# Column means of an 8192 x 8192 array: two-row loads up to group 59, another set of early blocks, and a last row group in four other pieces

## The chip, the cores and the metric

The kernel runs on one core of a Trainium2 chip. The time is the device time of one execution in microseconds (us); the runs shown are separate executions of the same program. The profile is one profiled execution of that program, with times counted from its first instruction.

The engines are named as the profile names them: PE is TensorE (PEld is its weight load), DVE is VectorE, ACT is ScalarE, POOL is GpSimd and SP is SyncE. A "q" behind the name, as in SPq, is the engine's instruction queue, where it waits or issues transfers.

## The reference

```python
def setup_inputs():
    return {"x": np.random.randn(8192, 8192).astype(np.float32)}

def reference(x):
    return np.mean(x, axis=0)
```

The input has 268 MB in fp32, the output 32 KB. Every element is read once and added.

## The kernel before

The 8192 rows are 64 *row groups* of 128 rows each, numbered 0 to 63 (the variable `g`); one row group fills the 128 partitions and has 8192 columns, cut into 16 *blocks* of `F = 512` columns. `W = 128` is a quarter of a block. A tile `bufs` holds six row groups: slots 0 to 3 take the loads in turn, slot 4 is called `both` and slot 5 `acc`.

**Loads.** SyncE issues all loads, in program order, from one queue; `load` (L75) sends one off as soon as the reader of its target slot has ended. First come two blocks of row group 60 into the tile `early`, then row groups 0 to 3 in one load, 4 and 5 in one load straight into `both` and `acc`, and five blocks of row group 63 into `early`. Row groups 6 to 55 are loaded in pairs, 56 to 59 one at a time, 60 with its first 14 blocks, 61 and 62 whole, and of row group 63 what is left in four pieces: blocks 4 to 7, 0 to 3, 14 and 15, and 8.

**Adds.** VectorE adds (`add`, L94; the instruction is L96). For a pair it writes the sum of both row groups to `both` and adds that to `acc`: two adds of 8192 columns. For a single row group it adds straight to `acc`. A no-op on ScalarE or GpSimd (L99) waits for the load and the add before it on VectorE's behalf, so that VectorE has one wait only. From row group 61, VectorE adds blocks 7 to 15 alone; row group 62 it does not add at all. GpSimd adds the early blocks to `acc` behind row groups 24 and 32 (L129) and three blocks of row group 62 at the end (L148).

**Products.** The sum over the 128 partitions is made by TensorE: a matmul with a 128 x 32 matrix of 1/8192 (`ones`) gives the column means of up to 512 columns. Block `i` goes to the 32-column strip `i % 4` of the array and to PSUM tile `banks[i // 4]`, so that four blocks can run on the four strips side by side. What was not added to `acc` is summed in PSUM: products of `acc`, row groups 61, 62 and 63 for the same columns go to the same place. The list `sums` gives their order, which is kept. Blocks 9 to 13, 14 and 15, and 8 are cut over all four strips (`spread`) into the PSUM tiles `wide`, `two` and `last`. There are 63 products.

**End.** ScalarE copies the PSUM tiles to `both` (L198), VectorE copies `last` to `tail` (L214). Five stores (L201) write the output, two of them issued by ScalarE and three by SyncE, the last one of `tail`. `landed` (L69) makes SyncE wait for loads and stores ahead of the end.

Of the kernel before, what the change touches and what calls it, by code (L numbers as in the profile page):

```python
# [9 lines left out]
def kernel(  # L10
# [2 lines left out]
    x: bass.AP,  # L13
    out: bass.AP,
):

    nc = tc.nc
    f32 = mybir.dt.float32
    M, N = x.shape  # L40
    P = nc.NUM_PARTITIONS
    F = 512
    W = F // 4
    G = M // P
    U = 6
    sync = mybir.DependencyInfo(mybir.DependencyClass.Sync, mybir.DependencyReason.DATA)

    sb = ctx.enter_context(tc.tile_pool(name="sb", bufs=1))
    psp = ctx.enter_context(tc.tile_pool(name="psum", bufs=1, space=bass.MemoryType.PSUM))
# [2 lines left out]
    both = bufs[:, U - 2, :]  # L52
    acc = bufs[:, U - 1, :]
    ones = sb.tile([P, 32], f32, name="ones")
    early = sb.tile([P, 7 * F], f32, name="early")
    tail = sb.tile([P, W], f32, name="tail")
    warm = sb.tile([P, 32], f32, name="warm")
    nc.gpsimd.memset(ones[:], 1.0 / M)  # L58
    ready = sb.tile([P, 1], f32, name="ready")
    tc.keep_in_program_order(  # L60
        nc.gpsimd.tensor_add(out=ready[:], in0=ones[:, 0:1], in1=ones[:, 1:2]))  # L61
    banks = [psp.tile([P, F], f32, name=f"bank{b}") for b in range(2)]
    wide = psp.tile([P, 2 * F], f32, name="wide")
    two = psp.tile([P, 2 * W], f32, name="two")
    last = psp.tile([P, W], f32, name="last")

    loads = []
# [1 line left out]
    def landed(*inss):  # L69

        nop = tc.keep_in_program_order(nc.sync.nop()).ins
        for o in inss:
            tc.add_manual_dep(nop, o.name, sync, reason="SyncE waits")

    def load(dst, src):  # L75
        ins = tc.keep_in_program_order(nc.sync.dma_start(out=dst, in_=src)).ins  # L76
        k = len(loads)
        over = loads[k - 8:k - 6] if k >= 8 and k % 2 == 0 else []
        tc.declare_no_dep(ins, group="loads", keep=over, reason="the reader of the buffer waited")
        for o in over:  # L80
            tc.add_manual_dep(ins, o.name, sync, reason="covers the next load too")
        tc.add_to_no_dep_group("loads", ins)
        loads.append(ins)
        return ins

    def rows(g, n=1):
        return x[g * P:(g + n) * P, :]

    def load_rows(g, u, n):
        return load(bufs[:, u:u + n, :], rows(g, n).rearrange("(p j) c -> p j c", j=n))  # L90
# [2 lines left out]

    def add(dst, a, b, dmas):  # L94

        ins = nc.vector.tensor_add(out=dst, in0=a, in1=b).ins  # L96
        if dmas and adds:
            waiter = nc.scalar if len(adds) % 8 > 1 else nc.gpsimd
            nop = joins[waiter] = tc.keep_in_program_order(waiter.nop()).ins  # L99
            for o in dmas + adds[-1:]:  # L100
                tc.add_manual_dep(nop, o.name, sync, reason="the no-op waits")
            for group in ("loads", "adds"):
                tc.declare_no_dep(ins, group=group, reason="the no-op waited")
            tc.add_manual_dep(ins, nop.name, sync, reason="waits for both at once")
        elif adds:
            tc.declare_no_dep(ins, group="loads", reason="the add ahead waited")
        tc.declare_no_dep(ins, group="early", reason="the no-op waited, or the add behind it")
        tc.add_to_no_dep_group("adds", ins)
        adds.append(ins)

    load(early[:, 5 * F:], rows(G - 4)[:, 14 * F:])
    first, second = load_rows(0, 0, 4), load_rows(4, 4, 2)
    load(early[:, :5 * F], rows(G - 1)[:, 9 * F:14 * F])
    add(bufs[:, 2:4, :], bufs[:, 2:4, :], bufs[:, 0:2, :], [first])
    add(bufs[:, 4:6, :], bufs[:, 4:6, :], bufs[:, 2:4, :], [second])
    add(acc, acc, both, [])
    tc.keep_in_program_order(nc.scalar.copy(out=warm[:], in_=ones[:]))  # L117
    ahead = []
    g = 6
    while g < G - 8:  # L120
        u = (g + 2) % 4
        dma = load_rows(g, u, 2)
        add(both, bufs[:, u, :], bufs[:, u + 1, :], [dma])
        add(acc, acc, both, ahead)
        ahead = []
        if g in (24, 32):
            lo, hi = (0, 4) if g == 24 else (4, 7)
            cols = slice((9 + lo) * F, (9 + hi) * F)
            ins = tc.keep_in_program_order(nc.gpsimd.tensor_add(  # L129
                out=acc[:, cols], in0=acc[:, cols], in1=early[:, lo * F:hi * F])).ins  # L130
            tc.add_to_no_dep_group("early", ins)
            ahead = [ins]
        g += 2

    while g < G - 4:
        row = bufs[:, (g + 2) % 4, :]
        add(acc, acc, row, [load(row, rows(g))])
        g += 1
    for lo, hi, loaded in [(0, 14, 14), (7, 16, 16)]:
        row = bufs[:, (g + 2) % 4, :]  # L140
        dma = load(row[:, :loaded * F], rows(g)[:, :loaded * F])
        cols = slice(lo * F, hi * F)
        add(acc[:, cols], acc[:, cols], row[:, cols], [dma])
        g += 1
    r61, r62, r63 = [bufs[:, (g + 1 + j) % 4, :] for j in range(3)]
    load(r62, rows(g))
    for cols in [slice(14 * F, 16 * F), slice(8 * F, 9 * F)]:
        joined = tc.keep_in_program_order(nc.gpsimd.tensor_add(  # L148
            out=acc[:, cols], in0=acc[:, cols], in1=r62[:, cols])).ins
    g += 1  # L150
    for lo, hi in [(4, 8), (0, 4), (14, 16), (8, 9)]:
        load(r63[:, lo * F:hi * F], rows(g)[:, lo * F:hi * F])

    sums = []

    def blocks(row, lo, hi):
        for i in range(lo, hi):
            sums.append((banks[i // 4], i % 4, 0, row[:, i * F:(i + 1) * F]))

    def spread(dst, row, lo, hi, part=slice(None)):  # L160
        n = (hi - lo) * W
        for c in range(0, n, F)[part]:
            for q in range(4):
                at = lo * F + q * n + c
                sums.append((dst, q, c, row[:, at:at + min(F, n - c)]))

    blocks(acc, 2, 5)
    blocks(acc, 0, 2)
    blocks(r61, 0, 7)
    blocks(acc, 5, 8)  # L170
    blocks(r62, 0, 8)
    spread(wide, acc, 9, 14, slice(1))
    blocks(r63, 4, 8)
    spread(wide, r62, 9, 14, slice(1))
    for row in (acc, r62):
        spread(wide, row, 9, 14, slice(1, 2))
    spread(two, acc, 14, 16)
    blocks(r63, 0, 4)
    spread(last, acc, 8, 9)
    spread(two, r63, 14, 16)  # L180
    spread(last, r63, 8, 9)
    for n, (dst, q, c, cols) in enumerate(sums):
        summed = tc.keep_in_program_order(nc.tensor.matmul(  # L183
            out=dst[32 * q:32 * q + 32, c:c + cols.shape[1]],
            lhsT=ones[:],
            rhs=cols,
            start=all((d is dst, k, at) != (True, q, c) for d, k, at, _ in sums[:n]),
            stop=all((d is dst, k, at) != (True, q, c) for d, k, at, _ in sums[n + 1:]),
            tile_position=(0, 32 * q),
            skip_group_check=True,  # L190
        )).ins

    res = both[:, :2 * F].rearrange("p (b c) -> p b c", b=2)
    res5 = both[:, 2 * F:2 * F + 5 * W]
    res2 = both[:, 4 * F:4 * F + 2 * W]

    def copy(dst, src):
        return tc.keep_in_program_order(nc.scalar.copy(out=dst, in_=src)).ins  # L198

    def store(engine, dst, src, *then):  # L200
        ins = tc.keep_in_program_order(engine.dma_start(out=dst, in_=src)).ins  # L201
        for o in then:
            tc.add_manual_dep(ins, o.name, sync, reason="follows that load")
        return ins

    def part(lo, hi):
        return out[lo * F:hi * F].rearrange("(q c) -> q c", q=4)

    copy(res[:, 1, :], banks[1][:])
    s1 = store(nc.scalar, part(4, 8), res[0:P:32, 1, :], loads[-4])  # L210
    copy(res5, wide[:, :5 * W])
    copy(res[:, 0, :], banks[0][:])
    copied = copy(res2, two[:])
    ended = nc.vector.tensor_copy(out=tail[:], in_=last[:]).ins  # L214
    landed(*joins.values())
    s5 = store(nc.sync, part(9, 14), res5[0:P:32, :], *loads[-7:-3])
    s0 = store(nc.sync, part(0, 4), res[0:P:32, 0, :])
    s2 = store(nc.scalar, part(14, 16), res2[0:P:32, :])
    store(nc.sync, part(8, 9), tail[0:P:32, :])
    landed(loads[-2], joined)  # L220
    landed(loads[-1], copied)
    landed(s0, s5)
    landed(s1, summed)
    landed(s2, ended)
    hold = tc.keep_in_program_order(nc.vector.nop()).ins
    tc.add_manual_dep(hold, s0.name, sync, reason="VectorE ends late")

# [29 lines left out]
```

## Time and profile before

| | us |
|---|---|
| median of 3 runs | 628.49 |
| lowest and highest | 628.24, 628.56 |
| span of the profiled execution, first to last instruction | 626.4 |
| median minus that span | 2.1 |
| VectorE busy | 529.3 (85%) |
| TensorE busy | 13.3 (2%) |
| HBM read | 268.44 MB, 429 GB/s over the span |

The profile does not list a device time of the profiled execution beside its span; the runs' median stands in for it. The table gives averages over the whole span. The busy share of an engine says how much work it has, not when the work can begin; the order of the last 80 us is read in the timeline, and the chain of waits says what ended last. DMA engines are busy in every slice of the page.

### The profile page before, as it was taken

The numbers are of one execution on the slowest core, as the hardware profiler recorded it, in microseconds if no ns is written. First come the engines' busy times: TensorE is split into PE (matmuls) and PEld (weight loads), VectorE is DVE, ScalarE is ACT, GpSimd is POOL, SyncE is SP. The second block draws the span as 40 slices with busy tenths as digits, with TensorE's granted clock in tenths as the row PEclk, the third lists the DMA queues.
The fourth block names the chain that finished last, engine by engine and source line by source line (L and its number), as shares of the span: only waits on it lengthen the run. The fifth ranks groups of instructions, "written<-read, shape, count | busy, mean of one in ns | idle before, by whom it ended". The sixth has DMA issues, their size and how long they took to land.

```text
span 626.4 us, 484 instructions
## 1 busy us (share of the span) xinstructions
PE 13.3 (2%) x126; PEld 4.0 (1%) x126; DVE 529.3 (85%) x60; ACT 3.7 (1%) x6; POOL 12.0 (2%) x10
## 2 busy tenths in 40 slices
PE   0000000000000000000000000000000000000008
PEld 0000000000000000000000000000000000000002
DVE  0028999998888998889998899888898888999992
ACT  0000000000000000000000000000000000000001
POOL 0000000000000000020000200000000000000002
PEclk9999999999999999999999999999999999999999
DMA  8999999999999999999999999999999999999997
GB/s 372 465 402 428 459 410 460 402 469 402 469 402 469 402 469 402 469 402 469 402 465 406 439 431 427 444 410 460 402 469 402 469 402 469 402 435 435 419 435 305
DMA packets 5930, 268.50 MB, mean 429 GB/s; under 512 B 660, under 2 KB 668, under 8 KB 1064
## 3 DMA queue, kind: packets, MB, share of 16 engines
q1 hardware_dynamic: 5912, 268.46, 99.3%
q8 instruction: 1, 0.02, 0.0%
q10 hardware_dynamic: 16, 0.01, 0.0%
q14 instruction: 1, 0.01, 0.0%
HBM read 268.44 MB, written 0.03 MB: 429 GB/s over the span
## 4 chain that ended last, share of the span: by engine, by line
DMA 59%; DVE 30%; another core or an unknown queue 10%; issue 0%; SPq 0%; ACTq 0%; PE 0%; POOL 0%; POOLq 0%
DMA bufs<-in_x_dram 59%; DVE bufs L96 30%; SPq L76 0%; ACTq L99 0%; PE last L183 0%; DVE tail L214 0%; POOL ready L61 0%; POOL ones L58 0%; POOLq L99 0%; POOLq L241 0%
## 5 line engine op out<-in xcount | busy, mean ns | idle before, releaser
L96 DVE TENSOR_TENSOR bufs<-bufs 128x8192 f32<-128x8192 f32 (+3 forms) x59 | 529.0, 8966 | 85.9 <-DMA bufs<-in_x_dram 43.0
L183 PE MATMUL bank<-bufs,ones 128*32 128x512 f32 x62 | 10.0, 716 | 610.3 <-DVE bufs L96 610.0
L129 POOL TENSOR_TENSOR bufs<-bufs,early 128x2048 f32<-128x2048 f32 (+1 forms) x2 | 7.9, 3954 | 348.5 <-DVE bufs L96 348.5
L148 POOL TENSOR_TENSOR bufs<-bufs 128x1024 f32<-128x1024 f32 (+1 forms) x2 | 3.6, 1824 | 258.9 <-DMA bufs<-in_x_dram 258.9
L214 DVE COPY tail<-last 128x128 f32<-128x128 f32 x1 | 0.3, 291 | 8.8 <-PE last L183 8.8
L183 PEld LDWEIGHTS bank<-bufs,ones 128*32 128x32 f32 x62 | 2.2, 121 | 616.4 <-issue 614.5
L198 ACT COPY bufs<-bank 128x512 f32<-128x512 f32 x2 | 1.2, 586 | 617.9 <-PE bank L183 617.9
L183 PE MATMUL wide<-bufs,ones 128*32 128x512 f32 (+1 forms) x32 | 2.5, 432 | 0.0
L117 ACT ACT_TABLE_LOAD x1 | 1.3, 1283 | 0.7 <-PEq L241 0.7
L183 PE MATMUL two<-bufs,ones 128*32 128x256 f32 x16 | 1.2, 380 | 0.0
L183 PEld LDWEIGHTS wide<-bufs,ones 128*32 128x32 f32 x32 | 1.0, 110 | 1.8 <-issue 1.8
L183 PE MATMUL last<-bufs,ones 128*32 128x128 f32 x16 | 0.8, 279 | 0.1
L198 ACT COPY bufs<-wide 128x640 f32<-128x640 f32 x1 | 0.7, 692 | 1.1 <-PE wide L183 1.1
L183 PEld LDWEIGHTS last<-bufs,ones 128*32 128x32 f32 x16 | 0.4, 109 | 1.2 <-issue 0.6
L183 PEld LDWEIGHTS two<-bufs,ones 128*32 128x32 f32 x16 | 0.4, 109 | 0.1
L198 ACT COPY bufs<-two 128x256 f32<-128x256 f32 x1 | 0.4, 372 | 0.1
L117 ACT COPY warm<-ones 128x32 f32<-128x32 f32 x1 | 0.2, 217 | 0.0
L61 POOL TENSOR_TENSOR ready<-ones 128x1 f32<-128x1 f32 x1 | 0.2, 193 | 0.1
L58 POOL MEMSET ones<- 128x32 f32 x1 | 0.1, 125 | 0.3 <-POOLq L241 0.3
L241 POOL MEMSET const-float32-0.0<- 128x1 f32 x1 | 0.1, 98 | 0.2 <-issue 0.2
L241 POOL MEMSET const-bfloat16-1.0<- 128x1 bf16 x1 | 0.1, 102 | 0.0
L241 POOL MEMSET const-uint8-127<- 128x1 uint8 x1 | 0.1, 102 | 0.0
(1 smaller groups left out, 0.1 us busy)
## 6 DMA issues: line engine op xcount, KB each, us to landing
bufs<-in_x_dram SPq DMA_DIRECT2D x6, 4096.0 KB, 20.4
bufs<-in_x_dram SPq DMA_DIRECT2D x1, 3584.0 KB
bufs<-in_x_dram SPq DMA_DIRECT2D x2, 1024.0 KB, 18.7
early<-in_x_dram SPq DMA_DIRECT2D x1, 1280.0 KB
early<-in_x_dram SPq DMA_DIRECT2D x1, 512.0 KB
bufs<-in_x_dram SPq DMA_DIRECT2D x1, 512.0 KB, 19.4
bufs<-in_x_dram SPq DMA_DIRECT2D x27, 29.9
bufs<-in_x_dram SPq DMA_DIRECT2D x1, 256.0 KB, 19.7
```

Of the source, the lines that this page charges most:

```text
L58: nc.gpsimd.memset(ones[:], 1.0 / M)
L61: nc.gpsimd.tensor_add(out=ready[:], in0=ones[:, 0:1], in1=ones[:, 1:2]))
L96: ins = nc.vector.tensor_add(out=dst, in0=a, in1=b).ins
L117: tc.keep_in_program_order(nc.scalar.copy(out=warm[:], in_=ones[:]))
L129: ins = tc.keep_in_program_order(nc.gpsimd.tensor_add(out=acc[:, cols], in0=acc[:, cols], in1=early[:, lo * F:hi * F])).ins
L148: joined = tc.keep_in_program_order(nc.gpsimd.tensor_add(out=acc[:, cols], in0=acc[:, cols], in1=r62[:, cols])).ins
L183: summed = tc.keep_in_program_order(nc.tensor.matmul(out=dst[32 * q:32 * q + 32, c:c + cols.shape[1]], lhsT=ones[:], rhs=cols, start=all(( ...
L198: return tc.keep_in_program_order(nc.scalar.copy(out=dst, in_=src)).ins
L214: ended = nc.vector.tensor_copy(out=tail[:], in_=last[:]).ins
L241: nc = _bacc.Bacc("TRN2", target_bir_lowering=False, num_devices=1)
```

## The change

Loads: the early blocks are the first six of row group 61 (two ahead of everything, four behind row group 5). Row groups 0 and 1 are loaded into `both` and `acc`, and all further ones up to 59 as pairs; row group 60 whole and alone; of row group 61 the ten blocks left; 62 whole; 63 whole, in pieces of 8, 4, 3 and 1 blocks.

Adds: row groups 2 and 3, then 4 and 5, are added as pairs of 16384 columns onto `both` and `acc`. Row groups 60 and (its ten blocks) 61 are added to `acc`; 62 and 63 are not added. GpSimd adds two early blocks behind row group 24, four behind 32, and none at the end.

Products: row group 62, then `acc`, then row group 63, with 16 blocks each; blocks 0 to 14 whole into four `banks`, block 15 as four quarters into `last`. These are 57 products.

End: four ScalarE copies, of the banks in order (the fourth with 96 partitions), one VectorE copy of `last`, and three stores, all by SyncE: 12 blocks, 3 blocks, 1 block. The waits of SyncE for loads stand partly ahead of the stores.

The diff, cut to its core:

```diff
-    early = sb.tile([P, 7 * F], f32, name="early")
+    E = 6
+    early = sb.tile([P, E * F], f32, name="early")
...
-    banks = [psp.tile([P, F], f32, name=f"bank{b}") for b in range(2)]
-    wide = psp.tile([P, 2 * F], f32, name="wide")
-    two = psp.tile([P, 2 * W], f32, name="two")
+    banks = [psp.tile([P, F], f32, name=f"bank{b}") for b in range(4)]
...
-    load(early[:, 5 * F:], rows(G - 4)[:, 14 * F:])
-    first, second = load_rows(0, 0, 4), load_rows(4, 4, 2)
-    load(early[:, :5 * F], rows(G - 1)[:, 9 * F:14 * F])
-    add(bufs[:, 2:4, :], bufs[:, 2:4, :], bufs[:, 0:2, :], [first])
-    add(bufs[:, 4:6, :], bufs[:, 4:6, :], bufs[:, 2:4, :], [second])
-    add(acc, acc, both, [])
+    def load_early(lo, hi):
+        load(early[:, lo * F:hi * F], rows(G - 3)[:, lo * F:hi * F])
+
+    sums2 = bufs[:, U - 2:, :]
+    load_early(0, 2)
+    first = [load_rows(0, U - 2, 2)]
...
-    g = 6
-    while g < G - 8:
+    for g in range(2, G - 4, 2):
         u = (g + 2) % 4
         dma = load_rows(g, u, 2)
+        if g < 6:
+            add(sums2, sums2, bufs[:, u:u + 2, :], [dma] + first)
+            first = []
+            if g == 4:
+                load_early(2, E)
+                add(acc, acc, both, [])
+            continue
         add(both, bufs[:, u, :], bufs[:, u + 1, :], [dma])
         add(acc, acc, both, ahead)
...
-    while g < G - 4:
-        row = bufs[:, (g + 2) % 4, :]
-        add(acc, acc, row, [load(row, rows(g))])
-        g += 1
-    for lo, hi, loaded in [(0, 14, 14), (7, 16, 16)]:
...
-    load(r62, rows(g))
-    for cols in [slice(14 * F, 16 * F), slice(8 * F, 9 * F)]:
-        joined = tc.keep_in_program_order(nc.gpsimd.tensor_add(
-            out=acc[:, cols], in0=acc[:, cols], in1=r62[:, cols])).ins
-    g += 1
-    for lo, hi in [(4, 8), (0, 4), (14, 16), (8, 9)]:
-        load(r63[:, lo * F:hi * F], rows(g)[:, lo * F:hi * F])
+    r60, r61, r62, r63 = [bufs[:, (G - 4 + 2 + j) % 4, :] for j in range(4)]
+    add(acc, acc, r60, [load(r60, rows(G - 4))])
+    cols = slice(E * F, N)
+    add(acc[:, cols], acc[:, cols], r61[:, cols], [load(r61[:, cols], rows(G - 3)[:, cols])])
+    load(r62, rows(G - 2))
+    for lo, hi in [(0, 8), (8, 12), (12, 15), (15, 16)]:
+        load(r63[:, lo * F:hi * F], rows(G - 1)[:, lo * F:hi * F])
...
-    blocks(acc, 2, 5)
-    blocks(acc, 0, 2)
-    blocks(r61, 0, 7)
-    blocks(acc, 5, 8)
-    blocks(r62, 0, 8)
-    spread(wide, acc, 9, 14, slice(1))
-    blocks(r63, 4, 8)
-    spread(wide, r62, 9, 14, slice(1))
-    for row in (acc, r62):
-        spread(wide, row, 9, 14, slice(1, 2))
-    spread(two, acc, 14, 16)
-    blocks(r63, 0, 4)
-    spread(last, acc, 8, 9)
-    spread(two, r63, 14, 16)
-    spread(last, r63, 8, 9)
+    blocks(r62, 0, 16)
+    blocks(acc, 0, 16)
+    blocks(r63, 0, 16)
...
-    copy(res[:, 1, :], banks[1][:])
-    s1 = store(nc.scalar, part(4, 8), res[0:P:32, 1, :], loads[-4])
-    copy(res5, wide[:, :5 * W])
-    copy(res[:, 0, :], banks[0][:])
-    copied = copy(res2, two[:])
+    for b in range(3):
+        copy(res[:, b, :], banks[b][:])
+    copied = copy(res[:96, 3, :], banks[3][:96])
     ended = nc.vector.tensor_copy(out=tail[:], in_=last[:]).ins
     landed(*joins.values())
-    s5 = store(nc.sync, part(9, 14), res5[0:P:32, :], *loads[-7:-3])
-    s0 = store(nc.sync, part(0, 4), res[0:P:32, 0, :])
-    s2 = store(nc.scalar, part(14, 16), res2[0:P:32, :])
-    store(nc.sync, part(8, 9), tail[0:P:32, :])
+    landed(loads[-5], set_up)
+    landed(*loads[-4:-2])
+    s0 = store(nc.sync, out[:12 * F].rearrange("(b q c) -> q b c", q=4, c=F), res[0:P:32, 0:3, :])
+    s3 = store(nc.sync, out[12 * F:15 * F].rearrange("(q c) -> q c", q=3), res[0:96:32, 3, :])
+    store(nc.sync, out[15 * F:].rearrange("(q c) -> q c", q=4), tail[0:P:32, :])
```

## The prediction

> **What bounds the kernel now.** I read the chain of waits first, then the timeline from the last paired load to the end, then the groups by shape for durations.
>
> ```profile
> 1.13 61.22 another core or an unknown queue
> ...
> 472.04 0.03 ACTq L99
> ...
> 549.44 0.04 ACTq L99
> ...
> 603.45 19.74 DMA bufs<-in_x_dram
> ...
> 623.23 0.47 PE last L183 x8
> ...
> 623.73 0.29 DVE tail L214
> ```
>
> Columns: start, length, what. The no-op on L99 at 549.44 marks the landing of pair 54/55. Two such marks lie four pairs apart: (549.44-472.04)/4 = 19.35 us a pair, or 0.605 us for one block (128 rows by 512 columns, 32 blocks in a pair). The chain ends in the landing of the last load at 623.2, eight small products, one VectorE copy and a store. So the load stream is the limit, and only 3.2 us stand behind its last byte. From 549.44 to that landing 121 blocks pass, 121 x 0.605 = 73.2 us against 73.75 measured: no hole, 0.55 us lost on small pieces at the end.
>
> The timeline, columns start, length, engine, line, operation, count, and the idle time before:
>
> ```profile
> 549.50 65.39 DVE L96 TENSOR_TENSOR bufs<-bufs 128x8192 f32<-128x8192 f32 x8 [1.93 <-ACTq L99]
> 609.98 6.01 PE L183 MATMUL bank<-bufs,ones 128*32 128x512 f32 x30 [609.98 <-DVE bufs L96]
> 611.71 0.20 PEld L183 LDWEIGHTS bank<-bufs,ones 128*32 128x32 f32 x7 [0.68 <-issue]
> 612.56 0.18 PEld L183 LDWEIGHTS bank<-bufs,ones 128*32 128x32 f32 x1 [0.66 <-issue]
> 613.41 0.16 PEld L183 LDWEIGHTS bank<-bufs,ones 128*32 128x32 f32 x5 [0.68 <-issue]
> 613.88 0.12 PEld L183 LDWEIGHTS bank<-bufs,ones 128*32 128x32 f32 x3 [0.31 <-issue]
> 616.28 1.92 PE L183 MATMUL bank<-bufs,ones 128*32 128x512 f32 x16 [0.28 <-DMA bufs<-in_x_dram]
> 618.02 1.04 PE L183 MATMUL wide<-bufs,ones 128*32 128x512 f32 x8
> 622.32 0.40 PE L183 MATMUL last<-bufs,ones 128*32 128x128 f32 x8
> 622.43 1.26 SPq L201 DMA_DIRECT2D out_dram<-bufs  x2
> 624.04 0.50 SPq L201 DMA_DIRECT2D out_dram<-tail  x1
> ```
>
> The reader is to see three things. VectorE never pauses from 549.50 to 614.89: the single-row loads 56 to 59 land faster than it adds, so all its work is done 8.3 us before the last byte. TensorE starts at 609.98, before row 62 has landed (616.28), and gets 14 of its blocks done in that time. And TensorE has a price: a product appears as two passes, four blocks run side by side on the four 32-column strips, and a pass starts every 0.86 us up to 613.41, every 0.43 us afterwards. So a strip needs 1.72 us for a block in the first 3.43 us and 0.86 us later (616.28 to 618.02 is two blocks on each strip); a quarter block of 128 columns takes 0.22 us (622.32 to the next start at 622.54).
>
> ```profile
> L96 DVE TENSOR_TENSOR bufs<-bufs 128x7168 f32<-128x7168 f32 x1 | 7.6, 7625 | 0.1
> L96 DVE TENSOR_TENSOR bufs<-bufs 128x4608 f32<-128x4608 f32 x1 | 5.0, 4957 | 0.1
> L198 ACT COPY bufs<-bank 128x512 f32<-128x512 f32 x2 | 1.2, 586 | 617.9 <-PE bank L183 617.9
> ```
>
> The last number before the second bar is the mean in ns. A full 8192-wide add is 8.69 us (the 538.88 row of the same timeline).
>
> **The start of the change.** The bytes and the issuing queue stay. The first add needs rows 0 to 3, which land as before (42.99 in the timeline), now as two loads. The first add frees its source at 60.25, when SyncE issues the next pair; rows 4 and 5 land at 62.35 and the early blocks behind them, now four instead of five, end at 62.35 + 4 x 0.605 = 64.8. So 4.5 us of queued work cover the next load where 5.1 did. From the first issue at 0.74 to the flow of data takes about 2.35 us (98 blocks up to 62.35, 98 x 0.605 = 59.3, flow from 3.1), so the stream stays full; without cover it would cost those 2.35 us, and once more at the next buffer. I take nothing. The GpSimd adds of early blocks lengthened a VectorE add from 8.7 to 11.2 and 10.1 us in the chain; VectorE idles 1.93 us a pair and the stream runs ahead, so this stays hidden, at most 2.5 + 1.4 us if it did not. One early block fewer is loaded ahead, so pair 54/55 lands 0.6 us earlier, at 548.84.
>
> **The pairs at the end.** This is the costly part. Pair 56/57 lands at 568.2, pair 58/59 at 548.84 + 2 x 19.35 = 587.54, say 587.6. Only then can VectorE add them: two adds of 8.69 and the no-op's 0.06, to 605.1. Row 60 follows (8.69 and 0.1) to 613.9, and ten blocks of row 61: between 4.96 us for nine and 7.63 for fourteen, so 5.5, to 619.45. The waits of 1.9 us at both pairs, which the single rows had not, and the order put the end of the adds 4.55 us behind the present 614.89. Row 60's and 61's buffers come free at about 577 and row 62's and 63's at 596.4; row 61 ends on the wire at about 603.5, so 7 us of cover and no hole in the stream.
>
> **TensorE.** Row 62 lands five blocks earlier than now, because row 63 brings 16 blocks behind it instead of 11: 616.25 - 5 x 0.607 = 613.2. (0.607 is the mean of the last 110 blocks before it, 66.8 us.) TensorE starts there, not at 609.98. Each of three rows now costs a strip up to four blocks and a quarter. Two floors follow. By throughput: 613.25 + 2 slow blocks x 1.72 + 10 x 0.86 + 3 x 0.22 = 625.95. By the adds: at 619.5 strip 2 still has blocks 6, 10, 14 and a quarter of the sums and 2, 6, 10, 14 and a quarter of row 63, 7 x 0.86 + 2 x 0.22 = 6.5, so 626.0. The two agree, which makes the sum firm: to miss it on the low side both must fail. Now the products end 0.5 us after the last byte; then they end 2.8 us after it. The smaller last loads (8, 4, 3 and 1 blocks, landing at about 618.1, 620.5, 622.5 and 623.2) are all there before TensorE wants them, so that split is worth nothing.
>
> **Copies and stores.** Block 14 ends a quarter before the last product, at 625.75; the copy of the fourth bank starts 0.2 us later (pass end and release, as between 622.76 + 0.38 and 623.23 now) at 625.95 and takes 0.59: 626.54. The copies of banks 0 to 2 follow their blocks and end at about 625.7, and the first store is issued 625.7 to 626.3 (0.64 or 0.51, the two in the row of 1.26). The store of bank 3 is issued at 626.55 for 0.51, and the store of the last block, whose copy has ended by 626.45, stands behind it on SyncE: 627.1. Now it is issued at 624.04, because ScalarE issues its neighbour at the same time. That is 3.06 us later: 2.4 from TensorE, the rest from the fourth copy and the shared queue. From that issue to the end of the span is 2.36 us now (624.04 to 626.4); the same stores of 512 B chunks, so carried over. The extra waits on SyncE ahead of the first store are for loads that have landed by then, 0.05 us each, before 625.7: free. Dropped GpSimd adds (3.6 us at 616.5) and dropped copies lie off the path: nothing.
>
> Sum: span 626.4 + 3.06 = 629.45. The median of the runs, 628.49, is 2.1 above the span; carried over, 631.5.
>
> **A rule against the row.** The slow stretch lasted 3.43 us here, from the first pass to 613.41; the granted clock in the profile's windows is 1.00 throughout and does not show it. The Trainium skill (TensorE: Matmul & The Clock Gate, Part 1) says that the array runs at half clock until it was busy for one window of 3.4 us, that the window runs freely, and that the change comes around 4 us, half a microsecond either way. By that rule the stretch may be a little longer, and half of what is added would be lost: 0.3 us at 4 us, an estimate from that page. The sum goes by the row.
>
> **Rivals.**
> *Longer slow stretch.* TensorE starts at another moment, and the half speed may end later. For: the trace has only one start. Every slow pass more costs 0.43. Bounds: none more, or the stretch doubled, four passes, 1.7 us: 633.2.
> *The stream runs ahead (not slower).* Place: the start, and rows 56 to 61. If the two-row first loads hid the 2.35 us before the flow, and pairs kept 0.605 instead of 0.607 for 110 blocks (0.25), every landing, add and product would move 2.6 us earlier: 628.9, no measurable change. It decides from 1.8 us on, since a measurement of this kernel can tell about 0.2%, 1.26 us, from no change. Against: the first issue stays where it is, and nothing shortens the way to the first byte. Adds and TensorE would have to gain together, as both floors are at 626.
> *The stream runs dry.* If a load needs more than 4.5 us of cover, both early buffers leave holes; priced at up to 2.35 each, 634 to 636. Against: 5.1 us left none.
> *The edit does not do what it says.* Loads, products and stores are each kept in program order, so rows land and are multiplied as written. The one freedom is that strips run side by side: a strip could run ahead of its neighbours by one block, 0.86 us, which gives 630.6 and lies inside the forecast's ends.
>
> **How the numbers follow.** The forecast, 631.5, has 0.75: its own ends are 630.4 (adds and start 0.6 earlier, the fourth copy's store overlapped for 0.5) and 632.3. The longer slow stretch, 632.3 to 633.2, has 0.14; the stream ahead 0.05, of which 0.04 within 0.2% and 0.01 for more than its rows price; the dry stream 0.06. The range 630.4 to 633.2 leaves out the last two. Slower by over 0.2%: 0.95.
>
> **What would show it.** VectorE pauses about 1.9 us before 568.2 and 587.6 and ends its adds near 619.4. TensorE's first product starts near 613.2, released by a load and not by VectorE; passes go from 0.86 to 0.43 apart after some 3.4 us; the last product ends near 626.1, and the chain's last DMA step is row 58/59's, not the last load's, with VectorE and TensorE behind it. Three SyncE stores lie at 625.7, 626.55 and 627.1. I am wrong if the adds end before 617.5, if products end by 624.3, or if the last load lands more than 1 us away from 623.2.

## The result and the profile after

The changed kernel takes 631.87 us (median of 5, 631.50 to 632.94); the kernel before takes 628.40 (5 runs beside it). The ratio is 1.0057, with a 95% interval of 1.0045 to 1.0069. The forecast was 631.5. In a second series (the control below) it takes 632.80 against 628.23, ratio 1.0071 (1.0058 to 1.0083). The profiled execution is the longest of the first five: 632.94, with a span of 630.8.

The chain of waits of the changed kernel, columns start, length, what:

```profile
587.37 0.03 ACTq L76
...
596.14 16.73 DMA bufs<-in_x_dram
...
612.97 5.56 PE bank L139 x25
...
626.16 0.63 PE bank L139 x3
...
626.82 0.58 ACT bufs L152
```

The chain no longer ends in the last load. Its last wait for data is the one for row 62, a load that SyncE issued at 596.14, when an add released the slot, and that landed at 612.88. From there TensorE works without a gap of more than 0.11 us up to 626.8, and behind it come only a copy and the stores.

The timeline of the same execution:

```profile
568.06 17.42 DVE L73 TENSOR_TENSOR bufs<-bufs 128x8192 f32<-128x8192 f32 x2 [1.93 <-ACTq L76]
587.42 31.81 DVE L73 TENSOR_TENSOR bufs<-bufs 128x8192 f32<-128x8192 f32 x4 [1.95 <-ACTq L76]
...
612.97 6.07 PE L139 MATMUL bank<-bufs,ones 128*32 128x512 f32 x27 [612.97 <-DMA bufs<-in_x_dram]
613.79 0.23 PEld L139 LDWEIGHTS bank<-bufs,ones 128*32 128x32 f32 x4 [0.63 <-issue]
...
617.21 0.22 PEld L139 LDWEIGHTS bank<-bufs,ones 128*32 128x32 f32 x3 [0.63 <-issue]
618.06 0.22 PEld L139 LDWEIGHTS bank<-bufs,ones 128*32 128x32 f32 x3 [0.63 <-issue]
...
618.86 0.13 PEld L139 LDWEIGHTS last<-bufs,ones 128*32 128x32 f32 x3 [0.57 <-issue]
...
619.28 0.13 PEld L139 LDWEIGHTS last<-bufs,ones 128*32 128x32 f32 x3 [0.30 <-issue]
...
626.59 0.40 PE L139 MATMUL last<-bufs,ones 128*32 128x128 f32 x6
...
626.59 1.61 SPq L155 DMA_DIRECT2D out_dram<-bufs  x2
...
627.06 0.29 DVE L160 COPY tail<-last 128x128 f32<-128x128 f32 x1 [7.82 <-PE bank L139]
628.30 0.56 SPq L155 DMA_DIRECT2D out_dram<-tail  x1
```

VectorE stops for 1.93 and 1.95 us ahead of the two last pairs and ends its adds at 587.42 + 31.81 = 619.23 (614.89 before). TensorE starts at 612.97, released by a load; its weight loads, which go with the passes, are 0.85 us apart up to 618.06 and 0.80 up to 618.86, and only then 0.43. By the starts of the passes the slow stretch, from the first pass to the last that comes more than 0.7 us behind the one before it, lasts 5.88 us (612.97 to 618.85). The products end at 626.59 + 0.40 = 626.99. The last store is issued at 628.30 (624.04 before).

### The profile page after: what moved, and what is told of

Read it like the earlier page. It is cut to its first block, busy times and chain, and to the rows that moved or that the text cites. A ratio compares the mean times of both kernels' runs of the same rounds, so it can differ in the third digit from the quotient of the medians.

```text
span 630.8 us, 448 instructions
## 1 busy us (share of the span) xinstructions
PE 14.0 (2%) x114; PEld 5.3 (1%) x114; DVE 529.8 (84%) x60; ACT 3.8 (1%) x6; POOL 7.4 (1%) x8
## 4 chain that ended last, share of the span: by engine, by line
DMA 66%; DVE 28%; another core or an unknown queue 3%; PE 2%; issue 0%; SPq 0%; ACT 0%; ACTq 0%; POOLq 0%
DMA bufs<-in_x_dram 66%; DVE bufs L73 28%; PE bank L139 2%; SPq L53 0%; PE last L139 0%; ACT bufs L152 0%; ACTq L76 0%; POOLq L76 0%
## 5 line engine op out<-in xcount | busy, mean ns | idle before, releaser
L73 DVE TENSOR_TENSOR bufs<-bufs 128x8192 f32<-128x8192 f32 (+2 forms) x59 | 529.5, 8975 | 89.7 <-POOLq L76 54.0
L139 PE MATMUL bank<-bufs,ones 128*32 128x512 f32 x90 | 13.8, 729 | 613.0 <-DMA bufs<-in_x_dram 613.0
L111 POOL TENSOR_TENSOR bufs<-bufs,early 128x1024 f32<-128x1024 f32 (+1 forms) x2 | 6.8, 3416 | 349.9 <-DVE bufs L73 349.9
L139 PEld LDWEIGHTS bank<-bufs,ones 128*32 128x32 f32 x90 | 4.7, 129 | 619.4 <-issue 617.9
L152 ACT COPY bufs<-bank 128x512 f32<-128x512 f32 (+1 forms) x4 | 2.3, 585 | 622.8 <-PE bank L139 622.8
L139 PE MATMUL last<-bufs,ones 128*32 128x128 f32 x24 | 2.7, 287 | 0.0
```

The costliest lines, as they stand in the source:

```text
L73: ins = tc.keep_in_program_order(nc.vector.tensor_add(out=dst, in0=a, in1=b)).ins
L111: ins = tc.keep_in_program_order(nc.gpsimd.tensor_add(out=acc[:, cols], in0=acc[:, cols], in1=early[:, cols])).ins
L139: summed = tc.keep_in_program_order(nc.tensor.matmul(out=dst[32 * q:32 * q + 32, :], lhsT=ones[:], rhs=cols, start=all((d is dst, k) != (T ...
```

## Experiments

All times are medians of 5 or more runs, beside runs of the kernel before; a ratio is to that kernel, with its 95% interval. L numbers differ from kernel to kernel. Each run has one trace, of one execution; the slow stretch of TensorE is measured in it as above.

**The changed kernel again**, as control.

> The changed kernel once more, beside the next three. Median 631.9 (631.5 to 632.9). In the profiled run of the changed kernel the passes of TensorE were 0.85 us apart for 5.9 us, and its time was the longest of five. If the length of that stretch makes the spread, this profile has a shorter stretch and a shorter time, or a stretch near 6 us and a time near 633: time = about 630.5 + half of what the stretch has over 3.4 us, or more.

Measured: 632.80 (632.14 to 633.17). Two series of the same kernel thus differ by 0.93 us in the median, so medians alone do not tell smaller differences between the series. The profiled execution took 632.14. Its timeline:

```profile
587.77 31.81 DVE L73 TENSOR_TENSOR bufs<-bufs 128x8192 f32<-128x8192 f32 x4 [1.94 <-ACTq L76]
...
613.32 4.98 PE L139 MATMUL bank<-bufs,ones 128*32 128x512 f32 x27 [613.32 <-DMA bufs<-in_x_dram]
...
627.57 0.57 SPq L155 DMA_DIRECT2D out_dram<-tail  x1
```

```profile
616.71 0.22 PEld L139 LDWEIGHTS bank<-bufs,ones 128*32 128x32 f32 x4 [0.63 <-issue]
617.26 0.13 PEld L139 LDWEIGHTS bank<-bufs,ones 128*32 128x32 f32 x3 [0.33 <-issue]
```

The passes change pace at 616.71, 3.39 us after the start instead of 5.88, and the time of this execution is 0.8 us shorter, its last store 0.73. Half of the 2.49 us is 1.25, but row 62 landed later here and TensorE started 0.35 later. By its start and its pace alone TensorE would end at 626.1 (the sum is in the next section); it ends at 626.27, since now the adds, which end at 619.58, are the later floor: one product of the sums starts only at 619.64. So between these two executions the pace of TensorE counts most; that it makes the spread of all is not shown, as the other executions have no trace. The expected formula (630.5 plus half of what goes beyond 3.4) is too low: 630.5 against 632.14 measured.

**Rows 56 to 59 one at a time again.**

```diff
-    for g in range(2, G - 4, 2):
+    for g in range(2, G - 8, 2):
...
+    for g in range(G - 8, G - 4):
+        row = bufs[:, (g + 2) % 4, :]
+        add(acc, acc, row, [load(row, rows(g))])
```

> Changed kernel, but row groups 56 to 59 loaded and added one at a time, as before. Two floors theory (adds and TensorE each hold the end near 626): the adds end 4 us earlier, near 615.3, and the time does not move, 631.9 +- 0.6, as TensorE still starts at 612.9 with 12.75 blocks a strip. Rival, the late adds alone set the end: 4 us less, near 628. Rival, the clock alone: 631.9 as well.

Measured: 631.61 (631.14 to 632.26), ratio 1.0055 (1.0042 to 1.0067); the intervals of this run and the control overlap.

```profile
583.86 31.89 DVE L73 TENSOR_TENSOR bufs<-bufs 128x8192 f32<-128x8192 f32 x4
...
613.14 4.47 PE L143 MATMUL bank<-bufs,ones 128*32 128x512 f32 x27 [613.14 <-DMA bufs<-in_x_dram]
...
626.88 0.56 SPq L159 DMA_DIRECT2D out_dram<-tail  x1
```

The adds end at 583.86 + 31.89 = 615.75, 3.8 us earlier than in the control, and the last store comes 0.69 earlier, not 3.8. TensorE still starts at 613.1, with as much to do; its slow stretch was 2.53 us here, 0.86 shorter than in the control, which is 0.43 of the 0.69. That late adds alone set the end is refuted.

**TensorE at full pace when row 62 lands.** 32 products of row 61 into a PSUM tile that nobody reads, ahead of all others.

```diff
+    for i in range(32):
+        c = (E + i % 8) * F
+        tc.keep_in_program_order(nc.tensor.matmul(
+            out=spare[32 * (i % 4):32 * (i % 4) + 32, :], lhsT=ones[:], rhs=r61[:, c:c + F], ...))
```

> Changed kernel, plus 32 products of row group 61 into a PSUM tile that nobody reads, ahead of the products of row group 62, so that TensorE is busy from about 603 to 611. Two floors theory: TensorE runs passes 0.43 us apart from row 62 on, waits for the adds at about 618.6 and still ends near 626: 631.3 (631.0 to 631.7), and the runs lie closer together than 631.5 to 632.9. Rival, the slow stretch alone costs the time: 629.5 or less. Rival, late adds alone: 631.9 with the same spread.

Measured: 631.80 (631.31 to 632.21), ratio 1.0055 (1.0043 to 1.0068).

```profile
587.80 31.81 DVE L74 TENSOR_TENSOR bufs<-bufs 128x8192 f32<-128x8192 f32 x4 [1.94 <-ACTq L77]
603.65 8.91 PE L141 MATMUL spare<-bufs,ones 128*32 128x512 f32 x64 [603.65 <-DMA bufs<-in_x_dram]
...
613.31 3.21 PE L145 MATMUL bank<-bufs,ones 128*32 128x512 f32 x27 [0.75 <-DMA bufs<-in_x_dram]
...
619.66 2.33 PE L145 MATMUL bank<-bufs,ones 128*32 128x512 f32 x17 [0.79 <-DVE bufs L74]
...
627.60 0.56 SPq L161 DMA_DIRECT2D out_dram<-tail  x1
```

Eight blocks a strip warm the array up; from 613.31 the passes are 0.43 apart, TensorE runs out of work and waits for the adds (the release is VectorE), and goes on at 619.66, just behind their end at 587.80 + 31.81 = 619.61; the last store is issued at 627.60, in the control at 627.57. The slow stretch alone does not set the end either. The spread, 0.9 us against 1.0 in the control, hardly shrank; that part of the expectation failed.

**Both edits together.**

> Both edits of the two runs before: single row groups 56 to 59, and the 32 products that nobody reads. Two floors theory: only here both floors fall; the products end at 612.95 + 12 x 0.86 + 0.66 + 0.2 = 624.1, 1.9 us earlier than the floor of the adds: 629.5 (629.0 to 630.0). Rivals with one cause: no better than the better of the two runs before.

Measured: 631.32 (631.18 to 631.78), ratio 1.0050 (1.0037 to 1.0064). The expected 629.5 was missed by 1.8 us.

```profile
613.01 3.21 PE L149 MATMUL bank<-bufs,ones 128*32 128x512 f32 x27 [0.81 <-DMA bufs<-in_x_dram]
...
623.46 1.06 PE L149 MATMUL bank<-bufs,ones 128*32 128x512 f32 x6 [0.37 <-DMA bufs<-in_x_dram]
...
626.05 0.56 SPq L165 DMA_DIRECT2D out_dram<-tail  x1
```

Here both floors did fall: the last store is issued at 626.05, 1.5 us earlier than in the control. But TensorE now waits for loads (0.37 us at 623.46), which came late, and from the last store's issue to the end of the span it takes 3.35 us, where it took 2.5 in the three others of this series. In both runs with 32 extra products the traces have a packet of instructions (queue q8) crossing the DMA engines at 618, and by the landing events one of the 16 engines delivers its share of the pieces behind it 1.2 us after the other fifteen. In the changed kernel this packet comes at 623.6. A run further down tests this by itself.

**Same 57 products, both floors lowered by order.** Rows 56 to 59 one at a time, and the products of blocks 0 to 5 of the sums first.

```diff
-    blocks(r62, 0, 16)
-    blocks(acc, 0, 16)
+    blocks(acc, 0, E)
+    blocks(r62, 0, 16)
+    blocks(acc, E, 16)
```

> Changed kernel with row groups 56 to 59 loaded and added one at a time and the products of blocks 0 to 5 of the sums ahead of row group 62. Same 57 products, none added. Two floors theory: TensorE starts at 610.0 and the adds end at 615.5, both floors fall, and the products end 0.2 to 1.6 us behind the last load; 630.0 (629.4 to 630.9). Rival, the changed kernel is held by something else (stores, the start of the load stream): 631.3 or more, as with the 32 extra products.

Measured: 630.45 (629.21 to 630.90), ratio 1.0030 (1.0019 to 1.0041), inside the expected range. The interval lies below the control's.

```profile
610.29 7.80 PE L144 MATMUL bank<-bufs,ones 128*32 128x512 f32 x39 [610.29 <-DVE bufs L73]
...
624.94 0.29 DVE L165 COPY tail<-last 128x128 f32<-128x128 f32 x1 [9.21 <-PE bank L144]
626.19 0.56 SPq L160 DMA_DIRECT2D out_dram<-tail  x1
```

TensorE starts at 610.29, on an add, and ends at 624.9, 1.4 us earlier than in the control although its slow stretch lasted 5.9 us here. What is left to the kernel before is 1.2 us of products (24.9 against 23.7) and 0.7 us between the last ScalarE copy and the last store (624.71 to 626.19, against 623.23 to 624.04).

**The pairs alone, in the kernel before.**

```diff
-    while g < G - 8:
+    while g < G - 4:
```

> Kernel before, with row groups 56 to 59 as two pairs, nothing else. Theory: adds end at 588.15 + 17.4 + 7.6 + 5.0 + 0.2 = 618.35 instead of 614.9, and TensorE, whose block 7 of the sums waits for them ahead of all products of row groups 62 and 63, ends 1.6 to 2.5 us later: 630.4 (629.9 to 631.0). Rival, pairs cost nothing since VectorE idles anyway: 628.3.

Measured: 631.53 (631.22 to 631.78), ratio 1.0050 (1.0037 to 1.0062). The size is 0.5 us over the expected range.

```profile
588.10 30.21 DVE L96 TENSOR_TENSOR bufs<-bufs 128x8192 f32<-128x8192 f32 x4 [1.93 <-ACTq L99]
...
613.40 7.92 PE L183 MATMUL bank<-bufs,ones 128*32 128x512 f32 x46 [613.40 <-DVE bufs L96]
...
626.57 0.29 DVE L214 COPY tail<-last 128x128 f32<-128x128 f32 x1 [8.26 <-PE last L183]
```

The adds end at 618.31, as worked out. TensorE starts later too, at 613.40 instead of 609.98, since its first products are of the sums and wait for the add of row 60: in this kernel the pairs move both floors. The slow stretch (5.1 us in this trace) and the product of block 7, which waits for the adds ahead of rows 62 and 63, let the products end at 626.5. This one line costs 3.1 us, where the whole change costs 3.5 and 4.6 in its two series. So it is enough by itself; but undoing it in the changed kernel gives back only 1.2 us against the control (0.3 against the first series), since there TensorE starts with row 62 and not with the sums.

**Instructions as DMA traffic.** The kernel before with 32 small products (128 x 32, read by nobody) at its very start.

> Kernel before, with 32 small products (128 x 32, read by nobody) at the very start. In the two runs with 32 extra products a 16 KB packet of instructions crossed the DMA engines at about 618, took 1.0 us, and one of the 16 engines then landed its share of the last loads 1.2 us late; without them it comes at 622.3 to 623.6. If that packet is fetched after so many TensorE instructions and costs its engine 1 us, it comes at 616 to 619 here, the last load lands at about 624.3 and the time is 629.4 (629.1 to 629.8). Rival, the late landing had another cause: 628.3.

Measured: 629.61 (629.15 to 629.86, 11 runs), ratio 1.0018 (1.0010 to 1.0027). A line of the DMA queues in the window 616 to 621 (packets, MB, share of 16 engines), which the kernel before does not have there, and two of the timeline:

```profile
q8 instruction: 1, 0.02, 1.3%
```

```profile
622.42 1.06 PE L189 MATMUL bank<-bufs,ones 128*32 128x512 f32 x8 [0.74 <-DMA bufs<-in_x_dram]
...
625.11 0.50 SPq L207 DMA_DIRECT2D out_dram<-tail  x1
```

1.3% of 16 engines over 5 us is 1.04 us of one engine. The adds and the first products are where they were, but now TensorE waits 0.74 us for a piece that landed late, and the last store is issued at 625.11 instead of 624.04. So the packet, moved into the end of the load stream, costs 1.1 us. That explains the late loads in the run of both edits. Why that run's end was longer by 0.85 as well was not tested; its trace has an 8 KB packet of instructions (queue q14) at 627.1, before its last store has landed, where the three others of the series have it after. Four of the five landing events of that store stand by 627.7, the fifth at 628.5.

**The shared store queue.**

```diff
-    s3 = store(nc.sync, out[12 * F:15 * F]...
+    s3 = store(nc.scalar, out[12 * F:15 * F]...
```

> Changed kernel, but the store of blocks 12 to 14 issued by ScalarE instead of SyncE. In the traces of the changed kernel the store of the last block is issued 1.25 us after VectorE begins its copy, because it stands behind two stores on SyncE. If that queue costs time, the last store comes 0.6 to 0.9 us earlier and the time falls by 0.5 to 0.9 against the changed kernel (632.8 and 631.9 in two series), to 631 to 632.2. Rival, the end waits for the landing of the store of blocks 12 to 14 anyway: no change.

Measured: 632.14 (631.49 to 632.58), ratio 1.0060 (1.0047 to 1.0072). No difference can be told from the changed kernel's 1.0057 and 1.0071.

```profile
626.17 0.70 SPq L155 DMA_DIRECT2D out_dram<-bufs  x1
...
626.97 0.56 SPq L155 DMA_DIRECT2D out_dram<-tail  x1
627.01 1.35 ACTq L155 DMA_DIRECT2D out_dram<-bufs  x1
```

Two lines of the kernel before, then two of the run with the pairs alone:

```profile
620.60 1.07 ACTq L201 DMA_DIRECT2D out_dram<-bufs  x1
...
623.63 0.51 ACTq L201 DMA_DIRECT2D out_dram<-bufs  x1
```

```profile
626.75 0.52 ACTq L201 DMA_DIRECT2D out_dram<-bufs  x1
626.89 0.50 SPq L201 DMA_DIRECT2D out_dram<-tail  x1
```

The last store leaves SyncE 0.33 us after VectorE's copy has begun (1.25 before), but ScalarE's issue, begun at nearly the same time, takes 1.35 us: as long as SyncE's two had taken one after the other (0.56 and 0.78). So nothing is gained. That the two issues hold each other up is not shown: in the run with the pairs two issues lie side by side and take 0.52 and 0.50. What the traces do show is that ScalarE's first store takes 1.07 us in the kernel before, with no other issue beside it, and its second 0.51. Here the store is ScalarE's first, and 0.78 + 0.56 is 1.34. How much the shared queue is worth by itself stays open.

**Three blocks over four strips.** Blocks 12 to 14 as 384 columns on each strip.

```diff
-            if i < 15:
+            if i < 12:
...
+            elif i == 12:
+                for q in range(4):
+                    at = i * F + q * 3 * W
+                    sums.append((three, q, row[:, at:at + 3 * W]))
```

> Changed kernel, but blocks 12 to 14 cut over all four strips (384 columns each) instead of lying whole on strips 0 to 2, so that a strip has 3 whole blocks, three quarters and one quarter a row, and their store has 4 rows of 1536 B instead of 3 of 2 KB. Two floors theory: a strip saves a quarter block a row, 0.21 us each: 0.43 us on the floor of the adds, 0.65 on TensorE's; the store of 3 rows took 0.78 us to issue where one of 4 rows took 0.51. Sum 0.7 (0.4 to 0.9) less than the changed kernel, whose medians were 631.9 and 632.8: 631.6 (630.9 to 632.2). Rival, products are not on the path: no change.

Measured: 631.31 (631.17 to 631.67), ratio 1.0048 (1.0036 to 1.0061), in the expected range. That range holds the changed kernel's 631.87 as well, so the number alone does not decide.

```profile
612.91 4.84 PE L144 MATMUL bank<-bufs,ones 128*32 128x512 f32 x24 [612.91 <-DMA bufs<-in_x_dram]
...
625.30 1.35 SPq L160 DMA_DIRECT2D out_dram<-bufs  x2
...
626.75 0.50 SPq L160 DMA_DIRECT2D out_dram<-tail  x1
```

The products end at 625.49, with a slow stretch of 4.2 us; the two first stores take 1.35 us together instead of 1.61, where a store of four rows (0.55) replaces one of three (0.78).

**The start.** Row groups 0 to 3 of the kernel before in two loads of two.

> Kernel before, with row groups 0 to 3 loaded by two loads of two instead of one load of four, nothing else. If the start of the change costs or brings nothing, 628.4 (628.0 to 628.8), and the second add begins near 62.4 as before. Rival, shorter first loads start the stream earlier or leave a hole: the marks of the pairs move and the time with them, by up to 2.35 us either way.

Measured: 628.95 (628.50 to 629.07, 11 runs), ratio 1.0008 (0.9999 to 1.0017). The medians differ by 0.56 us, more than expected, though the interval takes in no change. Four lines of its chain, and one of its DMA queues between 470 and 482:

```profile
62.43 0.04 POOLq L99
...
471.81 0.04 ACTq L99
...
511.37 0.03 ACTq L99
...
550.07 0.03 ACTq L99
```

```profile
q14 instruction: 1, 0.01, 0.2%
```

The mark at 62.43 stands at 62.35 in the kernel before, so the start neither gained nor lost. The marks at 471.81, 511.37 and 550.07 stand there at 472.04, 510.75 and 549.44: the stream was 0.2 us ahead, then 0.6 behind. In between, at 476, lies one 8 KB packet of queue q14, and in every load that lands behind it one DMA engine is 0.83 to 0.86 us late, up to the end. The kernel before has that packet at 626.0, behind its last store, and the changed kernel at 629.9. That every execution of this kernel has it in the stream is not shown.

## Why the prediction was right

**The mechanism held.** The forecast named two floors, TensorE's start and the end of the adds, that stand at nearly the same time. Undoing either one alone leaves the last store within 0.7 us of the control (627.57 to 626.88 and 627.60); undoing both brings it to 626.05 and 626.19. TensorE's floor can be checked, where the adds were not the later one, in four traces with the forecast's own terms and the slow stretch of each trace: start + 12.75 x 0.86 (with three blocks spread, 12 x 0.86) + half of the slow stretch + 0.16 for the last pass gives 627.0, 626.5, 625.5 and 625.5 for the changed kernel, the store by ScalarE, the single rows and the spread; measured 627.0, 626.6, 625.6 and 625.5. The floor of the adds is seen in the run with 32 extra products, where TensorE ran out of work: 6.7 us from their end to the last product's (forecast 6.5). In the control the same 6.7 behind 619.58 give the 626.27 measured.

**Step by step**, for the profiled execution (span 630.8 against 629.45 worked out):

- The adds: forecast 619.45, measured 619.23. Pair 58/59: forecast 587.54, measured 587.37. Both pauses are there.
- Row 62 and TensorE's start: 613.25 forecast, 612.97 measured (-0.28).
- The slow stretch: 3.43 forecast, 5.88 here, which is half of 2.45 = +1.23. This is the rival of the longer stretch, which named 633.2; the execution took 632.94. The control's stretch was 3.4 again.
- From the fourth copy to the last store: forecast 1.15, measured 626.82 to 628.30 = 1.48, +0.33. This term was mis-sized: the store of three rows took 0.78 to issue, not 0.51.
- From the last store to the end: 2.36 forecast, 2.5 measured, +0.14. Outside the span: 2.1 both times.

These give 629.45 - 0.28 + 1.23 + 0.33 + 0.14 = 630.9. In the control, where the stretch was as forecast, the fourth copy began 0.13 late (626.08 against 625.95), the last store came 0.34 later behind it and the end 0.12: 629.45 + 0.59 = 630.0, measured 630.1. The four other executions of the first series, 631.5 to 631.9, have spans near 629.7; they have no trace, so which of these terms was smaller there is not shown.

**What was wrong.** The text said that the chain's last DMA step would be the pair's load. It was row 62's. In the profiled execution the longer slow stretch lifted TensorE's floor to 627.0, 1.1 us above that of the adds (619.23 + 6.7); in the control, where the floors lie within 0.2 us, the chain still runs over row 62. Two floors that agree are firm on the low side alone, as the text said: on the high side the later one is enough, and both medians lie there, the second series (632.80) in the band that was given to the longer stretch, though its one trace shows 3.4 us. As the pace of TensorE changes between executions, now the one floor and now the other is the later, which may be why lifting one alone moved the median (single rows, 1.2 us less than the control, with intervals that overlap, but 0.3 less than the first series). A slip without weight: the row of 30 passes ahead of row 62 in the kernel before is 15 blocks, not 14; no sum uses it.

**The rule that was weighed.** The slow stretch was 3.4 us in five of the twelve traces, the kernel before among them, 2.5 in one and 4.2 to 5.9 in the other six, while the granted clock read 0.998 to 1.000. The Trainium skill (TensorE: Matmul & The Clock Gate, Part 1) has a freely running window of 3.4 us and a change near 4 us, half a microsecond either way. A length that changes from execution to execution, 5.9 and 3.4 us for the same kernel, fits a window that runs freely; the half microsecond does not fit, and the stretch of 2.5 us is shorter than one window.

**The rivals.** The stream did not run ahead and did not run dry: its marks at the start (62.43 with two-row loads) and at the last pair are where they were forecast, and the last load landed at 622.8 in the profiled execution and at 623.1 in the control, where 623.2 was forecast.

## What to carry to other kernels

When two engines in a row reach the end at the same time, price a change by the later of both floors, and expect little from removing one. Loads in larger groups cost nothing in the stream (with the pairs alone the last load landed at 622.9, in the kernel before at 623.2) but hand the adder its last work later; at the end of a stream, small loads that are added as they land keep the tail short. And keep the matrix engine's last work started early: what it has to do after the last big landing counts at its slow pace first.

## What the runs showed of the hardware

- Instructions are DMA traffic: one packet of 16 KB held one of 16 DMA engines for 1.0 us, and when 32 extra products moved it from 622.6 to 618.8, into the load stream, the time rose by 1.1 us (629.61 against 628.47). In the kernel before it starts 0.6 us ahead of the last load's landing at 623.2, and no engine lands late.
- The slow pace of TensorE at its start lasted between 2.5 and 5.9 us in twelve traces, and 5.9 and 3.4 us in two of the same kernel.
- A store of three rows took 0.78 us to issue, stores of four rows 0.50 to 0.57 when they were not the first on their engine. ScalarE's first store of four rows took 1.07 us, its second 0.51.
